# RWKV-7 mixer of a two-layer trunk: chunk loads, PSUM hand-over and the order of paired matmuls

## The chip, the cores and the metric

The kernel runs as one program on one core of a Trainium2 chip. The metric is device microseconds of one execution. Engines are named as in the profile: PE is TensorE, PEld its weight loads, DVE is VectorE, ACT is ScalarE, POOL is GpSimd, SP is SyncE, which here only issues DMAs. A letter q behind an engine (SPq) marks its instruction queue.

## The reference

The network has two layers on 1024 tokens of width 1024: layer 0 mixes with an RG-LRU block, layer 1 with RWKV-7 time mixing; each layer then has cross-attention into 256 memory tokens and a squared-ReLU MLP. The change lies in the RWKV-7 mixer (16 heads of 64):

```python
w_log = -softplus(-(w0 + tanh(xw @ w1) @ w2)) - 0.5      # decay
a = sigmoid(a0 + (xa @ a1) @ a2)
def step(state, inp):                                     # one token, one head
    sa = einsum('bhij,bhj->bhi', state, a_t)
    state = state * w_t + sa * b_t + v_t * k_t
    y_t = einsum('bhij,bhj->bhi', state, r_t)
...
bonus = sum(rh * kh * r_k, axis=-1) * vh
out = (group_norm(y) + bonus) * g
return out @ w_o
```

## The kernel before

Activations lie with channels on the partitions, in eight tiles f of 128 channels (two heads of 64 each, one on partitions 0 to 63, one on 64 to 127) by 1024 tokens. Large products go through `mm3` (L314 to L320): each fp32 operand is split by `split` (L228) into a rounded part and a rest, both fp32r, ACT making the first (L233) and DVE the second (L234), and three fp32r matmuls make one product. Products with few columns use plain fp32 matmuls. SBUF tiles of 128x1024 come from one pool, `u`, with 45 buffers.

The mixer runs in stages. The k stage makes for each f the decay and the gate a (`decay`, L1297): four `mm3` with 64 rows each, w from partitions 0 to 63 and a from 64 to 127, two halves of 512 tokens each, every product followed by a tanh on ACT (L1306); in the program both halves of w come first, then both of a. An r stage follows, and beside both a triangular solve on POOL and DVE, whose results `merge` (L1439) joins on PE. The v stage then makes v for [0, 1], 2, ..., 7. Its `evac_v` (L1526) copies v out of PSUM (L1529), turns it (L1545), forms the product pr of r, k and r_k (L1536), sums pr over the 64 channels of a head with a block matrix of ones as a plain fp32 matmul of 512 columns (L1562), multiplies by v (L1563), makes the gate g (`mm3`, L1566, L1567) and stores the results from SP (L1552, L1556, L1570). `early` loads pr and k ahead (L1575, L1577).

The scan runs over 16 chunks c of 64 tokens. Chunks are loaded from DRAM in pairs n: `load` (keys and b, L1598, four DMAs; a and r, L1601, two), `load_solved` (the solved triangle, L1612), `load_late` (v, L1625; the gates, L1629). `scan_gram` (L1644) makes the 128x128 Gram matrices of a chunk in two groups g of four q: for each q one plain fp32 matmul (L1652) per head h, on partitions 0 to 63 and 64 to 127, into two PSUM banks; `scan_mask` (L1662 on DVE, L1664 on ACT) masks them, `scan_keys` (L1676, L1677) transposes the scaled keys. In the loop over c the steps are `values` (L1757, L1759), `from_state` (L1769), `solved` (L1775, DVE L1777), `update` (L1782, DVE L1784), `output` (L1789, ACT L1791); `post_var` (L1688) and `post_norm` (DVE L1696) normalise the chunk before, `flip_out` (PE L1703, DVE L1708) transposes the one before that. In chunk c the Gram matrices, keys and masks of chunk c + 1 are made.

Tile's scheduler sets the order on each engine from the program's order, the data, free buffers and its own times. `self.line(name)` adds edges: what is issued in the block comes behind the last instruction of the block of that name before, on the same engine; the steps of the loop over c stand in the line "scan". `self.behind()` puts a block's instructions behind the last one issued so far on their engine.

[...] `psum_layout("mixed")` gives four single banks ("still") and two pairs; "banks" closes the pairs' pool and gives four more single banks. The scan uses "banks", and the output projection `tphase` behind it (`p = self.psum()`, L601) uses pairs, after "mixed".

Of the kernel before, what the change touches and what calls it, by code (L numbers as in the profile page):

```python
# [8 lines left out]
F32R = mybir.dt.float32r  # L9
# [1127 lines left out]
def rwkv_consts(self):  # L1137
    nc = self.nc
    c = self.const
    self.omu = c([128, 48], "omu")  # L1140
    nc.vector.tensor_scalar(self.omu, self.colv("mu", 48), -1.0, 1.0, ALU.mult, ALU.add)
    self.w0h = c([128, 8], "w0h")
    nc.vector.tensor_scalar(self.w0h, self.colv("w0"), 0.5, None, ALU.mult)
    self.a0h = c([128, 8], "a0h")
    nc.vector.tensor_scalar(self.a0h, self.colv("a0"), 0.5, None, ALU.mult)
    self.kah = c([128, 8], "kah")
    nc.vector.tensor_scalar(self.kah, self.colv("k_a"), 0.5, None, ALU.mult)
    self.kam = c([128, 8], "kam")
    nc.vector.tensor_scalar(self.kam, self.colv("k_a"), -1.0, 1.0, ALU.mult, ALU.add)
    self.nkk = c([128, 8], "nkk")  # L1150
    nc.vector.tensor_scalar(self.nkk, self.colv("k_k"), -1.0, None, ALU.mult)

    self.ind = c([128, 2], "ind")
    nc.gpsimd.memset(self.ind, 0.0)
    nc.gpsimd.memset(self.ind[0:64, 0:1], 1.0)
    nc.gpsimd.memset(self.ind[64:128, 1:2], 1.0)

    self.id64 = c([128, 64], "id64")
    nc.vector.tensor_add(self.id64, self.ident[:, 0:64], self.ident[:, 64:128])

    self.mask = c([128, 128], "mask")
    nc.gpsimd.memset(self.mask, 1.0)
    for h in range(2):
        r = slice(h * 64, h * 64 + 64)

        for i in range(2):
            m = self.mask[r, i * 64:i * 64 + 64]
            nc.gpsimd.affine_select(m, m, pattern=[[1, 64]], base=i - 1,
                                    channel_multiplier=-1, compare_op=ALU.is_ge, fill=0.0)
    self.db = c([128, 256], "db")  # L1170
    self.pc = c([128, 128], "pc")

    self.ones = c([128, 128], "ones")
    nc.gpsimd.memset(self.ones, 0.0)
    for h in range(2):
        nc.gpsimd.memset(self.ones[h * 64:h * 64 + 64, h * 64:h * 64 + 64], 1.0)

    self.center = c([128, 128], "center")
    nc.vector.scalar_tensor_tensor(self.center, self.ones, -1.0 / 64, self.ident, ALU.mult, ALU.add)

# [60 lines left out]
def rwkv(self, X, xt, lw_wa, lw_g, post, mid):  # L1241
    nc, I = self.nc, self.I
    mm = nc.tensor.matmul
# [17 lines left out]
    wa2 = self.split(raw)  # L1261
    xk, xr, xv = ([[], []] for _ in range(3))
    for hf in range(2):
# [13 lines left out]
        if hf:  # L1277
            h = maps[0][2]
# [18 lines left out]
    def decay(f):  # L1297
        cs = slice(f * 128, f * 128 + 128)
        c1 = lambda t: t[:, f:f + 1]
        lw, a = self.unit(), self.unit()  # L1300
        for t, r, b in ((lw, slice(0, 64), self.w0h), (a, slice(64, 128), self.a0h)):
            for hf in range(2):
                s = slice(hf * 512, hf * 512 + 512)
                p = self.bank()
                self.mm3(p, (wa2[0][r, cs], wa2[1][r, cs]), (hwa[0][r, s], hwa[1][r, s]), True, True)
                nc.scalar.activation(t[:, s], p, AF.Tanh, bias=c1(b), scale=0.5)  # L1306
        nc.vector.tensor_scalar(lw, lw, -LC, -LC, ALU.mult, ALU.add)
        if f > 1:
            nc.scalar.activation(a, a, AF.Copy, scale=0.5, bias=0.5)
        else:  # L1310
            nc.vector.tensor_scalar(a, a, 0.5, 0.5, ALU.mult, ALU.add)
        IP = self.unit()
        nc.vector.tensor_tensor_scan(IP, d01, lw, 0.0, ALU.mult, ALU.add)
        P = lw
        nc.scalar.activation(P, IP, AF.Exp)
        nc.scalar.activation(IP, IP, AF.Exp, scale=-1.0)
        nc.sync.dma_start(Pd[cs, :], P)
        nc.scalar.copy(self.pc.rearrange("p (c q) -> p c q", q=8)[:, :, f], P[:, 63::64])
        dk[f] = a, P, IP
# [206 lines left out]
    def evac_v(f, p):  # L1526
        cs = slice(f * 128, f * 128 + 128)
        vt = self.unit()
        nc.scalar.copy(vt, p)  # L1529
        if f == 1:  # L1530

            self.depth, self.ahead = DA
            with self.behind():
                self.advance(self.taken - 1)
        pr, kp = ld.pop(f)
        nc.vector.scalar_tensor_tensor(pr, pr, self.col("r_k", f), kp, ALU.mult, ALU.mult)  # L1536


        if f % 2 == 0:
            vk[:] = [self.unit() for _ in range(2)]  # L1540
        for e in range(2):
            pt = self.bank()
            for i in range(4):
                tt = e * 4 + i
                mm(pt[:, i * 128:i * 128 + 128], vt[:, tt * 128:tt * 128 + 128], self.center, start=True, stop=True)  # L1545
            nc.scalar.copy(vk[e].rearrange("p (t h g i) -> p t h g i", h=2, g=2, i=64)[:, :, :, f % 2, :],
                           pt.rearrange("p (t h i) -> p t h i", h=2, i=64))
            if f % 2 and e == 0:

                for d in range(2):  # L1550
                    for h in range(2):
                        nc.sync.dma_start(sv0[d][hr[1 - h], h * 512 + (f - 1) * 64:h * 512 + (f + 1) * 64],  # L1552
                                          vk[0].rearrange("p (t h i) -> p t h i", h=2, i=128)[hr[d], 0, h, :])
            if f % 2:
                for h in range(2):
                    nc.sync.dma_start(Vd[e * 512:e * 512 + 512, h, (f - 1) * 64:(f + 1) * 64].rearrange("(t p) i -> p t i", p=128),  # L1556
                                      vk[e].rearrange("p (t h i) -> p t h i", h=2, i=128)[:, :, h, :])
        g1 = self.unit()
        for e in range(2):
            s = slice(e * 512, e * 512 + 512)  # L1560
            bp = self.bank()
            mm(bp, self.ones, pr[:, s], start=True, stop=True)  # L1562
            nc.vector.tensor_mul(vt[:, s], vt[:, s], bp)  # L1563
            gp = self.bank()
            self.mm3(gp, (g2[0][:, cs], g2[1][:, cs]), (hg[0][:, s], hg[1][:, s]), True, True)
            nc.scalar.activation(g1[:, s], gp, AF.Copy, scale=self.col("gn_g", f))  # L1566
            nc.vector.scalar_tensor_tensor(vt[:, s], vt[:, s], self.col("gn_b", f), gp, ALU.add, ALU.mult)  # L1567
        for src, dst in ((g1, G1d), (vt, G2d)):
            for h in range(2):
                nc.sync.dma_start(dst[(f % 2) * 64:(f % 2) * 64 + 64, (f // 2) * 2 + h, :], src[h * 64:h * 64 + 64, :])  # L1570
# [73 lines left out]
    def scan_gram(c, g):  # L1644

        if c >= 16:
            return
        s = cst[c]
        s["pv", g] = [self.bank(h).rearrange("p (q w) -> p q w", q=4) for h in range(2)]
        for q in range(4):  # L1650
            for h in range(2):
                mm(s["pv", g][h][:, q, :], s["st"][g][hr[h], q].rearrange("p w t -> p (w t)"), s["mv"][hr[h], 4 * g + q],  # L1652
                   start=True, stop=True)

    def scan_mask(c, g):
        if c >= 16:
# [58 lines left out]
    for i, fs in enumerate(turns):  # L1715
        for f in turns[i + 1] if i < 6 else []:
            early(f)
        if fs[-1] >= 5:
            self.depth, self.ahead = min(2, 7 - fs[-1]), 0
        self.fphase(I["b_w_rkv"][0, 2], fs, xv, evac_v, spread=i == 0)  # L1720
        aside(len(TURNS) + 6 + i)
        if fs[-1] == LD:
            with self.behind():
                load(0)
        if fs[-1] == 6:
            load_solved(0)
    for c in range(2):
        scan_scale(c)
        for g in range(2):
            scan_gram(c, g)  # L1730
            scan_mask(c, g)
            scan_keys(c, g)
    load_late(0)
    self.psum_layout("banks")
    for h in range(2):
        nc.gpsimd.memset(cst[0]["sv"][hr[h], :, h, :], 0.0)
    for c in range(16):
        if c % 2 == 0:
            with (ExitStack() if c else self.behind()):
                load(c // 2 + 1)  # L1740
                load_solved(c // 2 + 1)
                load_late(c // 2 + 1)
        s = cst[c]
        sv, mv, pcc, xtc, pcs = s["sv"], s["mv"], s["pcc"], s["xt"], s["pcs"]
# [50 lines left out]
        todo = [(decayed, 0), (decayed, 1)] if c < 15 else []  # L1795
        if c:
            todo += [(scan_scale, c + 1)]
        todo += [(values, 0), (from_state, 0)]
        if c > 1:
            todo += [(flip_out, c - 2)]  # L1800
        todo += [(values, 1), (from_state, 1)]
        if c:
            todo += [(post_var, c - 1)]
        todo += [(solved, 0), (solved, 1)]
        if c:
            todo += [(scan_gram, c + 1, 0)]
        if c < 15:
# [14 lines left out]
    post_var(15)  # L1822
    post_norm(15)
    self.depth, self.ahead = 2, 3
    self.psum_layout("mixed")

    self.later += [lambda: flip_out(14), lambda: flip_out(15)]
    w = I["b_w_o"][0]
# [54 lines left out]
```

## Time and profile before

| | us |
|---|---|
| median of 3 runs | 2896.13 |
| lowest and highest run | 2890.81, 2898.02 |
| profiled execution | 2897.32 |
| its span from first to last instruction | 2895.6 |
| mean granted PE clock | 0.987 |
| PE busy in the span | 2804.9 (97%) |

The profiled execution is 1.7 us longer than its span, which is what lies around the first and the last instruction, and 1.2 us above the median. Shares of busy time are averages over many stages; the rows below take the stages of the mixer one by one.

### The profile page before, as it was taken

To read this page: it belongs to the slowest core of one execution; us is meant where nothing else is said; L and a number is where in the kernel's file an instruction comes from. 1 tells how busy PE (TensorE), PEld (TensorE's weight loads), DVE (VectorE), ACT (ScalarE), POOL (GpSimd) and SP (SyncE) were. 2 spreads that over 40 slices of the span, in tenths; PEclk is the share of its full clock that TensorE was granted. 3 is DMA by queue.
4 is the path that set the end of the run, shared out by engine and by line. 5 is a ranking of instruction groups with operands and counts; after the bars stand their busy time and mean duration, and the time that the engine had idled before them with its cause. 6 is when DMAs were issued, how large, how long until landed. Compare 5 with 4: busy or idle time off the path is not lost.

```text
span 2895.6 us, 42717 instructions
## 1 busy us (share of the span) xinstructions
PE 2804.9 (97%) x16955; PEld 2341.9 (81%) x16955; DVE 1834.2 (63%) x1995; ACT 1421.7 (49%) x2195; POOL 907.3 (31%) x962
## 2 busy tenths in 40 slices
PE   7999999999999999999999999999999999999998
PEld 6888788887888888887877777888788788888886
DVE  5577566657455577886675724775665645567778
ACT  5455354546454543347561634564463645454333
POOL 2000114023666500012288113753202276650001
PEclk9999999999999999999999999999999999999999
DMA  8212342323444654442657898952232354464443
GB/s 260 73 50 74 109 161 74 111 80 96 154 148 156 224 183 155 151 136 83 172 142 210 224 231 237 231 146 88 88 95 73 109 163 154 138 243 162 151 175 116
DMA packets 383592, 421.92 MB, mean 146 GB/s; under 512 B 91184, under 2 KB 294176, under 8 KB 383392
## 3 DMA queue, kind: packets, MB, share of 16 engines
q1 hardware_dynamic: 371360, 379.19, 43.5%
q0 software_dynamic: 11568, 39.41, 3.8%
q8 instruction: 133, 2.18, 0.3%
q14 instruction: 67, 0.55, 0.1%
q10 hardware_dynamic: 464, 0.59, 0.1%
HBM read 283.79 MB, written 134.74 MB: 145 GB/s over the span
## 4 chain that ended last, share of the span: by engine, by line
PE 86%; DVE 5%; ACT 3%; DMA 2%; issue 2%; SPq 1%; POOL 0%; DVEq 0%; POOLq 0%; ACTq 0%
PE q L318 17%; PE q L320 17%; PE q L319 17%; PE p L318 9%; PE p L320 9%; PE p L319 9%; DVE u L234 1%; PE q L1652 1%; ACT u L233 1%; PE q L386 1%; DMA u<-in_b_w_rkv 1%; DVE u L1199 1%; PE q L1545 1%; PE q L1769 1%; ACT u L930 1%
## 5 line engine op out<-in xcount | busy, mean ns | idle before, releaser
L234 DVE TENSOR_TENSOR u<-u,u 128x1024 fp32r<-128x1024 f32 (+1 forms) x594 | 799.3, 1378 | 353.9 <-ACT u L233 331.8
L233 ACT CAST u<-u 128x1024 fp32r<-128x1024 f32 (+1 forms) x594 | 582.2, 1019 | 416.3 <-DVE u L1042 224.7
L318 PE MATMUL q<-u,u 128*128 128x512 f32 (+2 forms) x1984 | 760.3, 386 | 15.4 <-ACT u L391 10.0
L319 PE MATMUL q<-u,u 128*128 128x512 f32 (+2 forms) x1984 | 759.6, 384 | 0.5 <-POOL u L366 0.5
L320 PE MATMUL q<-u,u 128*128 128x512 f32 (+2 forms) x1984 | 753.9, 384 | 0.8 <-DVE u L234 0.8
L318 PE MATMUL p<-u,u 128*128 128x512 f32 (+1 forms) x1472 | 557.0, 381 | 12.2 <-ACT u L233 5.4
L319 PE MATMUL p<-u,u 128*128 128x512 f32 (+1 forms) x1472 | 553.1, 376 | 3.7 <-DVE u L234 3.6
L320 PE MATMUL p<-u,u 128*128 128x512 f32 (+1 forms) x1472 | 552.6, 376 | 3.6 <-DVE u L234 3.6
L318 PEld LDWEIGHTS q<-u,u 128*128 128x128 f32 (+1 forms) x1984 | 373.6, 189 | 92.8 <-ACT u L391 10.9
L320 PEld LDWEIGHTS q<-u,u 128*128 128x128 f32 (+1 forms) x1984 | 373.9, 189 | 74.3 <-DVE u L234 1.0
L329 POOL TENSOR_SCALAR s<-s 128x1 f32<-128x1 f32 x98 | 39.0, 398 | 1258.3 <-ACT u L327 1256.7
L319 PEld LDWEIGHTS q<-u,u 128*128 128x128 f32 (+1 forms) x1984 | 374.2, 189 | 72.3 <-POOL u L366 1.0
L318 PEld LDWEIGHTS p<-u,u 128*128 128x128 f32 x1472 | 281.2, 191 | 66.4 <-ACT u L233 7.5
L319 PEld LDWEIGHTS p<-u,u 128*128 128x128 f32 x1472 | 281.3, 191 | 55.0 <-DVE u L234 6.7
L320 PEld LDWEIGHTS p<-u,u 128*128 128x128 f32 x1472 | 281.3, 191 | 54.7 <-DVE u L234 5.2
L440 POOL TENSOR_TENSOR u<-u,u 128x512 f32<-128x512 f32 x120 | 189.1, 1579 | 9.0 <-PE q L319 5.1
L1100 DVE TENSOR_TENSOR z<-z,q 128x512 f32<-128x512 f32 x192 | 130.5, 683 | 81.0 <-PE q L320 81.0
L318 PE MATMUL q<-z,u 128*128 128x512 f32 x320 | 124.7, 391 | 1.6 <-ACT u L233 1.6
L320 PE MATMUL q<-z,u 128*128 128x512 f32 x320 | 124.5, 390 | 1.1 <-DVE u L234 1.1
L319 PE MATMUL q<-z,u 128*128 128x512 f32 x320 | 124.6, 389 | 0.0
L441 POOL TENSOR_TENSOR u<-u 128x512 f32<-128x512 f32 x40 | 70.0, 1749 | 166.1 <-DVE u L234 63.7
L997 POOL TENSOR_TENSOR u<-u,u 128x512 f32<-128x512 f32 x32 | 44.2, 1381 | 177.0 <-ACT u L986 159.8
(247 smaller groups left out, 3334.6 us busy)
## 6 DMA issues: line engine op xcount, KB each, us to landing
u<-d SPq DMA_DIRECT2D x194, 512.0 KB, 4.7
d<-u SPq DMA_DIRECT2D x109, 512.0 KB, 3.5
d<-u POOLq DMA_DIRECT2D x68, 512.0 KB, 3.3
d<-u SPq DMA_DIRECT2D x132, 256.0 KB, 3.6
u<-in_m_w_up SPq DMA_DIRECT2D x64, 512.0 KB, 5.5
u<-in_m_w_down SPq DMA_DIRECT2D x64, 512.0 KB, 8.1
u<-in_c_w_kv SPq DMA_DIRECT2D x32, 512.0 KB, 6.5
u<-in_b_w_rkv SPq DMA_DIRECT2D x24, 512.0 KB, 6.2
```

The costliest lines, as they stand in the source:

```text
L233: self.nc.scalar.copy(hv, src)
L234: (eng or self.nc.vector).tensor_tensor(lv, src, hv, ALU.subtract)
L318: mm(o, ah, bh, start=first, stop=False, **kw)
L319: mm(o, ah, bl, start=False, stop=False, **kw)
L320: mm(o, al, bh, start=False, stop=last, **kw)
L329: nc.gpsimd.tensor_scalar(v, ss, 1.0 / n, eps, ALU.mult, ALU.add)
L386: nc.tensor.transpose(p[:, i * 128:i * 128 + 128], x[:, k * 128:k * 128 + 128], self.ident)
L440: sub = lambda o, x, y: nc.gpsimd.tensor_tensor(o, x, y, ALU.subtract)
L441: nc.gpsimd.tensor_tensor(s[:, a], f1[:, a], f1[:, b], ALU.add)
L930: nc.scalar.activation(e[:, s], p[:, s], AF.Exp, bias=mx[:, i:i + 1], scale=1.0 / 16.0, accum_out=sm[:, i:i + 1])
L997: tt(s1, r21, r22, ALU.add)
L1100: nc.vector.tensor_add(to_, to_, o)
```

## The change

- `decay` goes over the halves of the tokens first, takes two PSUM banks, and issues the three matmuls of w and of a in turn (w, a, w, a, w, a), each matmul in its own block of a line "decay".
- In `scan_gram` each matmul stands in its own block of a line "gram", so that they keep the program's order, which alternates between the heads.
- `evac_v` splits pr into two fp32r tiles and sums each with an fp32r copy of the ones (`ones_r`), accumulating in PSUM.
- `load(1)` moves from chunk 0 of the scan to the v stage, behind v tile 6; `load_solved(1)` stands behind the v stage; both were issued in chunk 0.
- In the loop over c `flip_out` moves from between the two groups of `values` to behind `solved`.
- `psum_layout("mixed")` moves from behind the scan to the start of chunk 15.

```diff
+    self.ones_r = self.cpool.tile([128, 128], F32R, name="ones_r", tag="ones_r")
+    nc.vector.tensor_copy(self.ones_r, self.ones)
...
-        for t, r, b in ((lw, slice(0, 64), self.w0h), (a, slice(64, 128), self.a0h)):
-            for hf in range(2):
-                s = slice(hf * 512, hf * 512 + 512)
-                p = self.bank()
-                self.mm3(p, (wa2[0][r, cs], wa2[1][r, cs]), (hwa[0][r, s], hwa[1][r, s]), True, True)
+        for hf in range(2):
+            s = slice(hf * 512, hf * 512 + 512)
+            ps = [self.bank() for _ in range(2)]
+            for n, (i, j) in enumerate(((0, 0), (0, 1), (1, 0))):
+                for p, r in zip(ps, hr):
+                    with self.line("decay"):
+                        mm(p, wa2[i][r, cs], hwa[j][r, s], start=n == 0, stop=n == 2)
+            for t, p, b in zip((lw, a), ps, (self.w0h, self.a0h)):
                 nc.scalar.activation(t[:, s], p, AF.Tanh, bias=c1(b), scale=0.5)
...
+        prs = self.split(pr)
...
-            mm(bp, self.ones, pr[:, s], start=True, stop=True)
+            for i in range(2):
+                mm(bp, self.ones_r, prs[i][:, s], start=i == 0, stop=i == 1)
...
-                mm(s["pv", g][h][:, q, :], s["st"][g][hr[h], q].rearrange("p w t -> p (w t)"), s["mv"][hr[h], 4 * g + q],
-                   start=True, stop=True)
+                with self.line("gram"):
+                    mm(s["pv", g][h][:, q, :], s["st"][g][hr[h], q].rearrange("p w t -> p (w t)"), s["mv"][hr[h], 4 * g + q],
+                       start=True, stop=True)
...
             load_solved(0)
+            load(1)
+    with self.behind():
+        load_solved(1)
...
     for c in range(16):
+        if c == 15:
+            self.psum_layout("mixed")
         if c % 2 == 0:
             with (ExitStack() if c else self.behind()):
-                load(c // 2 + 1)
-                load_solved(c // 2 + 1)
+                if c:
+                    load(c // 2 + 1)
+                    load_solved(c // 2 + 1)
                 load_late(c // 2 + 1)
...
-        todo += [(values, 0), (from_state, 0)]
-        if c > 1:
-            todo += [(flip_out, c - 2)]
-        todo += [(values, 1), (from_state, 1)]
+        todo += [(values, 0), (from_state, 0), (values, 1), (from_state, 1)]
         if c:
             todo += [(post_var, c - 1)]
         todo += [(solved, 0), (solved, 1)]
+        if c > 1:
+            todo += [(flip_out, c - 2)]
...
     self.depth, self.ahead = 2, 3
-    self.psum_layout("mixed")
```

## Rows read from the trace of the kernel before

**Rows 1.** The page: shares of the chain that ended last, by engine
```profile
PE 86%; DVE 5%; ACT 3%; DMA 2%; issue 2%; SPq 1%; POOL 0%; DVEq 0%; POOLq 0%; ACTq 0%
```
**Rows 2.** Windows: stretch, length, busy us (instructions) per engine, granted clock, DMA share, GB/s
```profile
1356.00:1464.00 108.00, 108.00 (x718) 86.32 (x716) 71.87 (x71) 69.16 (x94) 33.71 (x41) 0.98 0.57 155
...
1600.00:1764.00 164.00, 156.56 (x1398) 122.44 (x1397) 71.84 (x103) 74.17 (x106) 33.36 (x50) 0.98 0.83 221
1764.00:1924.00 160.00, 153.45 (x3088) 138.08 (x3086) 112.05 (x212) 86.93 (x360) 107.44 (x123) 0.98 0.98 226
1924.00:1949.00 25.00, 21.05 (x191) 16.93 (x188) 19.47 (x23) 17.93 (x52) 4.95 (x5) 0.86 0.37 106
1786.50:1793.40 6.90, 6.22 (x58) 5.58 (x59) 2.92 (x6) 0.89 (x2) 4.88 (x6) 0.51 0.98 228
1933.30:1940.10 6.80, 6.12 (x27) 4.77 (x24) 5.45 (x6) 6.00 (x21) 1.83 (x2) 0.50 0.29 93
...
1745.00:1760.00 15.00, 13.90 (x125) 10.97 (x126) 2.87 (x5) 4.71 (x7) 7.00 (x9) 1.00 0.47 142
```
**Rows 3.** Timeline of PE, decay matmuls: start, us, operation, count
```profile
1371.61 0.49 PE L318 MATMUL q<-u,u 64*128 64x512 f32 x1
...
1372.19 0.62 PE L318 MATMUL q<-u,u 64*128 64x512 f32 x2
...
1373.77 0.50 PE L318 MATMUL p<-u,u 128*128 128x512 f32 x1
...
1399.86 0.50 PE L318 MATMUL q<-u,u 64*128 64x512 f32 x1
...
1400.66 0.39 PE L318 MATMUL q<-u,u 64*128 64x512 f32 x1
1400.89 0.39 PE L319 MATMUL q<-u,u 64*128 64x512 f32 x1
...
1401.44 0.50 PE L319 MATMUL p<-u,u 128*128 128x512 f32 x1
```
**Rows 4.** Timeline of PE, Gram matmuls of the scan
```profile
1764.71 1.71 PE L1652 MATMUL q<-z,u 64*128 64x128 f32 x16
...
1809.48 1.16 PE L1652 MATMUL q<-z,u 64*128 64x128 f32 x16
...
1812.70 1.71 PE L1652 MATMUL q<-z,u 64*128 64x128 f32 x16
```
**Rows 5.** The chain in order of time, and ACT's timeline, both of the v stage
```profile
1669.68 0.86 PE q L1562 x2
...
1722.68 1.04 ACT L233 CAST u<-u 128x1024 fp32r<-128x1024 f32 x1 [10.76 <-DMA u<-in_b_w_rkv]
```
**Rows 6.** Timelines of PE and of SP's queue around chunks 1 and 2
```profile
1787.18 2.08 PE L1652 MATMUL q<-z,u 64*128 64x128 f32 x16 [3.73 <-issue]
...
1795.78 0.64 PE L1757 MATMUL q<-u,u 128*64 128x64 f32 x16
...
1780.49 6.25 SPq L1598 DMA_DIRECT2D u<-d  x4
...
1797.01 6.91 SPq L1598 DMA_DIRECT2D u<-d  x4
```
**Rows 7.** Timelines of PE, DVE and ACT in the loop over chunks
```profile
1807.32 0.69 PE L1757 MATMUL q<-u,u 128*64 128x64 f32 x16
...
1816.79 0.63 PE L1703 MATMUL q<-ident,u 128*128 128x128 f32 x4 [0.22 <-DVE u L1696]
...
1924.48 0.33 PE L1757 MATMUL q<-u,u 128*64 128x64 f32 x2 [0.41 <-ACT u L1664]
...
1805.13 0.77 DVE L1696 TENSOR_TENSOR u<-u,g 128x512 f32<-128x512 f32 x1
...
1811.30 1.77 DVE L1784 TENSOR_TENSOR u<-u,q 64x256 f32<-64x256 f32 x4 [0.29 <-PE q L1782]
...
1815.62 0.40 ACT L1664 COPY u<-z 64x256 f32<-64x256 f32 x1 [0.19 <-DVE u L1662]
```

## The prediction

> **What bounds the kernel now.** I read the page's chain first, then windows of the mixer's stages, then the timelines of the places that the change touches. PE is 86% of the chain that ended last [rows 1], so a microsecond taken from PE's queue counts wherever PE has no wait behind which it vanishes. The windows say where that is so. While the decays run, PE is busy 108.00 of 108.00 us; in the v stage 156.56 of 164, in the scan 153.45 of 160, and at the change to the output projection 21.05 of 25 [rows 2]. [...] The scan has a second candidate: its DMA share is 0.98 [rows 2].
>
> **Decays.** A decay is twelve matmuls of 64 rows by 512 columns. In the row's order two of one half of the partitions follow each other at 0.23 us (1400.66 to 1400.89), and six of them take 1.58 us to the next matmul, that is 6 x 0.23 = 1.38 and 0.2 for going in and out of the 64-row shape [rows 3]. Where w's second product meets a's first, a row of two appears, and twelve take only 2.16 us (1371.61 to 1373.77) instead of 2.96: a pair from the two halves of the partitions runs in the time of one [rows 3]. The trace has eight groups of six, three of twelve, one of nine (1.59) like the former and one of three (0.9): 12.6 + 6.5 + 1.6 + 0.9 = 21.6 us for eight decays. In turns, every matmul has its partner: 3 x 0.23 + 0.2 = 0.9 us for each half of the tokens, 16 x 0.9 = 14.4 us, or 8 x (6 x 0.23 + 0.2) = 12.6 if the halves stay together. The gain is 7.2 to 9.0 us; I take 7.2, since most groups stand alone now. If pairs are torn apart it falls to 5. Nothing is added on ACT. The work hidden beside is none: PE is full here, and the DMAs of this stage (share 0.57 [rows 2]) hold nothing up.
>
> [...]
>
> **Bonus sums.** Each of the 16 plain fp32 matmuls of 512 columns takes 0.86 us on the chain [rows 5]; two fp32r matmuls of the same size take 2 x 0.23 = 0.46 [rows 3]. That is 16 x 0.40 = 6.4 us off PE. The price is per v tile one cast on ACT (1.04 [rows 5]) and one subtraction on DVE, and two more `u` buffers. ACT is busy 74.17 of these 164 us and DVE 71.84 [rows 2], so they fit. But ACT works in order, and once it sits 10.76 us before a cast that waits for a weight's DMA [rows 5], with v tiles' evacuations behind it; one more cast in that queue is 1.0 us of PE's wait, and the first tile, where pr comes just ahead of its matmul, waits for cast and subtraction once. I take 4.5 us; the ends are 1 and 6.4.
>
> **Gram matrices.** Eight fp32 matmuls, 16 records, take 1.71 us in some groups and 1.16 in others [rows 4]. In the shorter ones both heads start together, in the longer ones one head's four come first. The difference is 0.55 us. Of 32 groups 17 have the longer order: the four of chunks 0 and 1 ahead of the loop (from 1764.71 [rows 4]), and the second group of each of the chunks 2 to 14, that of chunk 2 at the lower clock. The first four give 4 x 0.55 = 2.2 us.
>
> In the loop the gain meets the next bound. From values(0) of chunk 2 at 1795.78 to that of chunk 15 at 1924.48 there are 13 periods of 9.90 us [rows 6, 7]; in 12 of them 0.55 would come off PE, and 0.22 more where `flip_out` waits for `post_norm` [rows 7], which its new place ends. The loop through DVE and ACT is: update's additions start at 1811.30, the last mask's copy on ACT ends at 1816.02, so values(1) can start 4.8 us later; from values(1) at 1807.32 to those additions are 3.98 us, now without `flip_out`, which is 0.63 long and is put into just this stretch [rows 7]. 4.8 + 3.98 + 0.63 = 9.4 us. So this loop, not PE, sets the period, and the gain is 13 x (9.90 - 9.40) = 6.5 us. If `post_norm` (0.77 at 1805.13, then one more mask [rows 7]) comes ahead of the last mask, 0.68 is added and the gain is nothing; by PE's work alone it would be 12 x 0.55 and some of the 0.22, 8 us.
>
> **The second pair of chunks.** PE stands 3.73 us before chunk 2's first Gram matrices [rows 6], and of the 6.22 busy us in the window behind it, at clock 0.51, up to half, 3.1 us, is the price of the lower clock [rows 2]. What it waits for is in SP's queue: the four DMAs of `load(1)` are issued from 1780.49 on, behind the last v tile's stores [rows 6], and PE goes on 6.7 us after the first. In its new place `load(1)` is behind v tile 6, where from 1745 to 1760 the DMA share is 0.47 [rows 2], so it lands 20 us ahead of its use. The stall goes, 3.73 + 3.1 = 6.8 us. What is late next is pair 2: its first DMA goes out at 1797.01 and lands by the same 6.7 us at 1803.7, for matmuls at 1809.48 [rows 4, 6], 5.8 us early; these come 10 us sooner now, but the queue ahead of it is shorter by 6.25 us and `load_solved`, so some 3 us are left. Moved past on SP are the last tile's own loads and stores; the copies into the first chunk's state may slip by the 6.25 us of the four issues. I take 6.0; ends 0 and 6.8.
>
> **PSUM one chunk sooner.** From 1924 to 1949 PE is idle 25 - 21.05 = 3.95 us, and the half clock of 1933.30 to 1940.10 costs about half of its 6.12 busy us, 3 [rows 2]. With a pair of banks free during chunk 15 the projection's first matmuls can fill these gaps. But they need split weights, DVE is busy 19.47 of the 25 us and ACT 17.93 with them [rows 2], and chunk 15 has four banks in place of eight. I take 3.0; ends 0 and 6.9.
>
> **Sum.** 7.2 + 4.5 + 2.2 + 6.5 + 6.0 + 3.0 = 29.4 us off the profiled 2897.3, gives 2867.9. That execution lies 1.2 us above the median of the runs shown, so I forecast 2867. With the low ends (5, 1, 2.2, 0, 0, 0: 8.2 us) 2888, with the high ones (9.0, 6.4, 2.2, 8, 6.8, 6.9: 39.3 us) 2857.
>
> **Rivals.** (1) The scan is bound by its transfers. For: DMA share 0.98 and 226 GB/s over the stage, at best 5.8 us between landing and use [rows 2, 4, 6]. Then a shorter period only moves the wait: the stall reappears before the Gram matrices of chunk 4, and the loop's 6.5 and the stall's 6.0 are gone: 29.4 - 12.5 = 16.9, 2879. Against: from pair to pair the queue now gains on PE, with waits in it for buffers that PE frees.
>
> (2) The turns do not overlap, because the second bank is late or the scheduler puts other matmuls between: 7.2, 2.2 and 6.5 fall away, 13.5 are left, 2883. For: four banks. Against: both kinds of pairs are in the trace already [rows 3, 4].
>
> (3) `post_norm` stays ahead of the last mask: without the loop's 6.5, 2873.
>
> (4) Slower. The `u` pool runs short in the v stage: two buffers for pr per tile and four for `load(1)` and `load_solved(1)` stand while weights are still to be fetched, so a tile's weights come one tile late. Its price is the 10.76 us which ACT sits before such a cast [rows 5], of which PE sees the part that its own queue doesn't cover, 3.7 us as at chunk 2, and 3 us for the lower clock behind it. One such stall costs 6.7 us; five more use up the 29.4, and with all six of the single v tiles it is 40 against 29.4: 2907. It decides from the fifth stall on. Against: by v tile 6, where `load(1)` stands, no weights beyond tile 7 are to come, and the trace has one such stall in the stage.
>
> **Chances.** Forecast 0.58; (1) 0.15; (3) 0.12; (2) 0.10; (4) 0.05. The range from 2855 to 2888 takes in the first four with their own spread. A difference under 0.3%, 8.7 us, can't be told from no change: below 2887.4 is faster, to which the forecast gives nearly all of its chance, (1) and (3) nine tenths and (2) six tenths: 0.86. Slower 0.05, the rest, 0.09, is the same.
>
> **What would show it.** Decays: twelve matmuls or six in rows of two, 0.9 us per half. Bonus: 32 fp32r matmuls on the line of L1562, 0.46 us per pair. Gram: 1.16 us in all 32 groups. Loop: a period of 9.4 us, with DVE and ACT without a gap from update's additions to the last mask; 9.9 would be rival (3) or (1), and for (1) PE's waits would name a DMA. Stall: no idle time over 1 us and clock 1.00 through chunks 1 and 2. Hand-over: projection matmuls between chunk 15's. For (4): ACT's casts waiting for `in_b_w_rkv` in several tiles. The prediction is wrong if the gain is under 9 us, or if it is large but from a place that isn't in the sum, such as another order of the scheduler in a stage that the change doesn't touch.

## The result

The changed kernel takes 2889.96 us (median of 13 runs) against 2896.13 us before, a ratio of 0.9977 with a 95% interval of 0.9966 to 0.9987. So it is faster, but by 6.2 us where 29.4 were forecast. That is less than the 8.7 us that I took for the least that can be told from no change, and the time lies 2 us above the top of my range. Between the two profiled spans (2895.6 and 2886.8 us) the gain is 8.8 us. The views after that answer to those of before are these: the chain's shares on the page, then the windows by stage (stretch, length, busy us and instructions of each engine, granted clock, DMA share, GB/s).

```profile
PE 83%; DVE 5%; DMA 3%; ACT 3%; POOL 2%; SPq 2%; issue 2%; DVEq 0%; POOLq 0%; ACTq 0%
```
```profile
1352.00:1460.00 108.00, 107.40 (x733) 82.85 (x732) 72.58 (x74) 72.27 (x100) 31.54 (x40) 1.00 0.53 147
1492.00:1549.00 57.00, 42.80 (x226) 34.31 (x227) 50.30 (x45) 32.05 (x44) 52.09 (x57) 0.85 0.49 142
1608.00:1764.00 156.00, 144.99 (x1366) 117.31 (x1365) 79.33 (x109) 79.74 (x111) 33.39 (x50) 0.98 0.88 235
1764.00:1918.00 154.00, 146.91 (x3040) 130.36 (x3040) 109.51 (x208) 89.70 (x364) 104.36 (x122) 1.00 0.99 233
1918.00:1943.00 25.00, 23.08 (x270) 18.81 (x266) 22.37 (x29) 19.00 (x54) 8.73 (x8) 1.00 0.37 107
```

PE's share of the chain fell by 3 points to the benefit of POOL, DMA and SP's queue [rows 1]. The clock of 0.86 at the hand-over is 1.00 now [rows 2]. But the second row is a stretch that my rows do not hold, the change from the k to the r stage. The same stretch before:

```profile
1492.00:1549.00 57.00, 53.86 (x348) 43.91 (x347) 45.44 (x42) 28.17 (x38) 50.79 (x61) 0.97 0.61 174
```

PE is busy 11 us less there, does 226 matmuls instead of 348, and the clock is 0.85. Setting the same instruction of both traces side by side, place by place, gives this account (us, minus is a gain; the expectations quoted below still count 0.8 us of the last v tile among the Gram groups, hence their 4.3 and 2.0, and give the stall 4.8):

| place | forecast | measured in the trace |
|---|---|---|
| k stage with the decays | -7.2 | -4.1 |
| change from k to r, 1492 to 1549 | 0 | **+14.2** |
| rest of the r stage | 0 | -2.2 |
| v stage with the bonus sums | -4.5 | -5.1 |
| first four Gram groups | -2.2 | -1.2 |
| stall at chunk 2 | -6.0 | -3.9 |
| chunks 2 to 14 | -6.5 | -0.9 |
| last chunk and hand-over | -3.0 | -4.6 |
| behind it | 0 | -1.0 |
| sum | -29.4 | -8.8 |

### The profile page after: what moved, and what is told of

It is laid out like the page before. It is cut to its first block, busy times and chain, and to the rows that moved or that the text cites. A ratio compares the mean times of both kernels' runs of the same rounds, so it can differ in the third digit from the quotient of the medians.

```text
span 2886.8 us, 42719 instructions
## 1 busy us (share of the span) xinstructions
PE 2781.7 (96%) x16955; PEld 2319.8 (80%) x16955; DVE 1840.0 (64%) x2004; ACT 1431.4 (50%) x2203; POOL 912.7 (32%) x962
## 3 DMA queue, kind: packets, MB, share of 16 engines
q8 instruction: 133, 2.18, 0.3%
## 4 chain that ended last, share of the span: by engine, by line
PE 83%; DVE 5%; DMA 3%; ACT 3%; POOL 2%; SPq 2%; issue 2%; DVEq 0%; POOLq 0%; ACTq 0%
PE q L320 16%; PE q L318 16%; PE q L319 16%; PE p L318 9%; PE p L320 9%; PE p L319 9%; DVE u L234 2%; DMA u<-in_b_w_rkv 2%; ACT u L233 1%; PE q L1661 1%; PE q L386 1%; POOL u L1417 1%; POOL w L1415 1%; DMA u<-d 1%; DVE u L417 1%
## 5 line engine op out<-in xcount | busy, mean ns | idle before, releaser
L234 DVE TENSOR_TENSOR u<-u,u 128x1024 fp32r<-128x1024 f32 (+1 forms) x602 | 807.6, 1374 | 353.8 <-ACT u L233 327.1
L233 ACT CAST u<-u 128x1024 fp32r<-128x1024 f32 (+1 forms) x602 | 591.0, 1020 | 434.2 <-DVE u L1042 224.8
L318 PE MATMUL q<-u,u 128*128 128x512 f32 (+1 forms) x1952 | 745.4, 384 | 15.7 <-ACT u L391 10.0
L319 PE MATMUL q<-u,u 128*128 128x512 f32 (+1 forms) x1952 | 747.0, 383 | 1.7 <-DVE u L234 1.2
L320 PE MATMUL q<-u,u 128*128 128x512 f32 (+1 forms) x1952 | 741.2, 383 | 0.8 <-DVE u L234 0.8
L318 PE MATMUL p<-u,u 128*128 128x512 f32 (+1 forms) x1472 | 555.6, 380 | 25.8 <-DVE u L1332 10.2
L318 PEld LDWEIGHTS q<-u,u 128*128 128x128 f32 x1952 | 367.4, 188 | 89.3 <-ACT u L391 10.9
L319 PEld LDWEIGHTS q<-u,u 128*128 128x128 f32 x1952 | 367.5, 188 | 74.2 <-DVE u L234 3.1
L320 PEld LDWEIGHTS q<-u,u 128*128 128x128 f32 x1952 | 367.2, 188 | 72.7 <-DVE u L234 1.0
```

Of the source, the lines that this page charges most:

```text
L233: self.nc.scalar.copy(hv, src)
L234: (eng or self.nc.vector).tensor_tensor(lv, src, hv, ALU.subtract)
L318: mm(o, ah, bh, start=first, stop=False, **kw)
L319: mm(o, ah, bl, start=False, stop=False, **kw)
L320: mm(o, al, bh, start=False, stop=last, **kw)
```

## Where the 14 us went

ACT's timeline in that stretch, first after, then before. L1427 after and L1421 before are the copy in `solve_store(0)`; L233 are casts of the next stage's weights.

```profile
1482.16 2.09 ACT L1427 COPY u<-u 64x1024 f32<-64x1024 f32 x1 [12.61 <-POOL u L1417]
1484.15 1.05 ACT L233 CAST u<-u 128x1024 fp32r<-128x1024 f32 x1
1491.54 1.04 ACT L233 CAST u<-u 128x1024 fp32r<-128x1024 f32 x1 [6.34 <-DMA u<-in_b_w_rkv]
```
```profile
1482.50 2.08 ACT L1421 COPY u<-u 64x1024 f32<-64x1024 f32 x1 [11.47 <-POOL u L1411]
1484.45 2.01 ACT L233 CAST u<-u 128x1024 fp32r<-128x1024 f32 x2
```

In both kernels the copy waits for POOL, whose solve ends at 1482: what PE saves before that does not move POOL. Before, two casts follow at once. After, the second waits 6.34 us more for its weights. SP's queue says why, first after, then before (L1428 and L1422 store the solved chunk, L249 loads weights):

```profile
1477.19 0.58 SPq L1395 DMA_DIRECT2D d<-u  x1
1482.15 0.34 SPq L1428 DMA_DIRECT2D d<-u  x1
1484.27 0.48 SPq L1429 DMA_DIRECT2D d<-u  x1
1484.84 2.12 SPq L249 DMA_DIRECT2D u<-in_b_w_rkv  x2
```
```profile
1475.68 1.23 SPq L249 DMA_DIRECT2D u<-in_b_w_rkv  x1
...
1483.11 0.56 SPq L1422 DMA_DIRECT2D d<-u  x1
1484.60 0.48 SPq L1423 DMA_DIRECT2D d<-u  x1
1485.17 0.54 SPq L249 DMA_DIRECT2D u<-in_b_w_rkv  x1
```

Before, one of the two weight loads went out at 1475.68, ahead of the stores. After, the scheduler put the stores first; SP stands idle from 1477.8 until POOL is done, with both loads behind it. The late cast makes PE wait in its turn (1502.00, then four more waits of 0.7 to 1.6 us), with spells of 10.2 us, most of it idle, and 6.8 us at half clock (the granted clock is 0.50 from 1494.95 to 1505.19 and from 1532.50 to 1539.33):

```profile
1502.00 0.77 PE L318 MATMUL p<-u,u 128*128 128x512 f32 x1 [10.24 <-DVE u L1332]
```

My theory T1 was that the decays' shorter matmuls flip this order. Five runs stand for it or against it. All ratios below are to the kernel before; its own median moved between 2893.9 and 2897.3 us from series to series, so the ratios compare better than the times.

**e1_old_decay** undoes the decays.

```diff
-        for hf in range(2):
-            ps = [self.bank() for _ in range(2)]
-            ...
+        for t, r, b in ((lw, slice(0, 64), self.w0h), (a, slice(64, 128), self.a0h)):
+            for hf in range(2):
+                self.mm3(p, (wa2[0][r, cs], wa2[1][r, cs]), (hwa[0][r, s], hwa[1][r, s]), True, True)
```


> The changed kernel with the decays' matmuls put back as they were (three matmuls of one map, then three of the other); everything else of the change stays. Theory T1: the decays' shorter k stage let the order of SP's instructions flip, so that two weight loads of the r stage stand behind the stores of the first solved chunk, which wait for POOL; that loses 14.2 us between 1492 and 1547 us of the changed kernel's trace. With the old decays the second of these loads goes ahead of the stores again: k stage 4.1 us longer, the 14.2 us stall gone (0 lost there against the kernel before), the later gains (v stage 4.3, first Gram groups 2.0, chunk 2's stall 4.8, hand-over 4.6) stay: 2896.1 - 16.7, some 2880 (2876 to 2884). Rival R1 (the loss belongs to another edit, such as the buffers that the bonus sums' split parts or the constant of ones take): the loss stays and only the decays' gain goes, some 2894 (2891 to 2897).

2883.2 us, 0.9953 (0.9941 to 0.9966): taking a gain away made the kernel 6.7 us faster. In its trace one weight load goes ahead of the stores again (L1425 is the first store):

```profile
1477.46 0.74 SPq L249 DMA_DIRECT2D u<-in_b_w_rkv  x1
...
1484.53 0.56 SPq L1425 DMA_DIRECT2D d<-u  x1
```

**e2_only_decay** is the kernel before with the decays alone (the diff above, reversed).


> The kernel before with the decays' edit alone. T1: 4.1 us gained in the k stage, then 12 to 14 us lost in the change to the r stage: 2896.1 + 8 to + 10, some 2904 (2901 to 2907), slower than before by 0.3%, with weight casts of ACT waiting for a transfer near 1490 us of the trace. R1: the loss belongs to another edit and is not here, so that the decays' gain remains, some 2892 (2889 to 2894).

2900.7 us, 1.0021 (1.0011 to 1.0030): slower, by 6 us (forecast 8 to 10). ACT shows the same wait as after, and PE stands 9.98 us at 1502.46:

```profile
1482.84 2.08 ACT L1424 COPY u<-u 64x1024 f32<-64x1024 f32 x1 [12.59 <-POOL u L1414]
1484.82 1.06 ACT L233 CAST u<-u 128x1024 fp32r<-128x1024 f32 x1
1492.21 1.04 ACT L233 CAST u<-u 128x1024 fp32r<-128x1024 f32 x1 [6.34 <-DMA u<-in_b_w_rkv]
```

From 1488 to 1564 us its trace loses 11.2 us on the kernel before, where the changed kernel loses 14.2. So it is the decays' edit and no other; R1 falls. What in this edit turns the scheduler's order, the shorter time, the edges of the line "decay" or the second bank, was not tried.

**e3_store_later** gives out the stores one turn later.

```diff
-SL, SO, ST = (2, 5, 8, 9), (2, 5, 8, 9), (5, 8, 12, 13)
+SL, SO, ST = (2, 5, 8, 9), (2, 5, 8, 9), (6, 8, 12, 13)
```


> The changed kernel with the first solved chunk's copy and stores given out one turn later (the first number of ST 6 in place of 5), all of the change in place. T1: both weight loads of that turn go ahead of the stores and ACT's casts are not held up, the 14.2 us between 1492 and 1547 us go, and the 4.1 us of the decays stay: 2890.0 - 10 to - 14, some 2877 (2873 to 2882). R1: the loss has nothing to do with where the stores stand: 2890 (2886 to 2894).

2876.9 us, 0.9936 (0.9924 to 0.9948), as T1 has it.

**e4_before_later** is its control: the same line in the kernel before.


> The kernel before with the first solved chunk's copy and stores one turn later: the control for the run above. T1: the kernel before had one weight load behind the stores and its two casts ran late by no more than some 2 us of PE's idle time (gaps of 1.73 and 1.29 us at 1509 and 1526 us): 2893 to 2896, no change that can be told or a little faster. R1': if turning the stores later is worth 10 us by itself, whatever the decays do, this kernel is faster by as much: some 2885.

2898.3 us, 1.0006 (0.9995 to 1.0016): no difference. The edit is worth 12 (by the ratios) to 13 us only where the decays have turned the queue.

**e13_pool_queue** moves nothing but the queue of the two stores; ACT's order stays.

```diff
+        dma = (nc.sync if q else nc.gpsimd).dma_start
-        nc.sync.dma_start(Xd[q]...)
+        dma(Xd[q]...)
```


> The changed kernel (2890.0 us), the first solved chunk's stores issued by POOL, which solves it, in place of SP; its copy stays where it is, in front of ACT's two weight casts. Theory T1 (the head of SP's queue): the weight loads no longer stand behind a store that waits for POOL, the second cast runs right behind the copy, and the loss between 1492 and 1547 us goes although ACT waits 12 us for POOL's solve as before: 2877 (2873 to 2882), as with the stores one turn later. Rival R8 (the head of ACT's queue: the casts are late because the copy waits there): nothing moves, 2890 (2887 to 2893), and the run store later gained because it moved the copy too.

2882.1 us, 0.9957 (0.9943 to 0.9971), at the upper end of T1's span. The second cast follows at once although the copy still waits 11.9 us, PE's wait falls from 10.24 to 1.95 us, and at the end of that change the kernel is 11.0 us ahead of the changed one. Then it gives 5.3 us back, 3.9 of them where the first merge waits for the same store, which now stands behind the next solve in POOL's queue (issued at 1543.18):

```profile
1477.09 1.20 SPq L249 DMA_DIRECT2D u<-in_b_w_rkv  x2
```
```profile
1480.63 2.08 ACT L1427 COPY u<-u 64x1024 f32<-64x1024 f32 x1 [11.88 <-POOL u L1417]
1482.61 2.00 ACT L233 CAST u<-u 128x1024 fp32r<-128x1024 f32 x2
```
```profile
1492.91 0.47 PE L318 MATMUL p<-u,u 128*128 128x512 f32 x1 [1.95 <-DVE u L1332]
...
1571.49 0.28 PE L1455 MATMUL q<-u 32*32 32x32 f32 x2 [3.90 <-DMA u<-d]
```

So SP's queue carries 11 of the 14 us. This kernel trails e3 there by the other 3; they are probably the copy's, at the head of ACT's queue, but no run moves the copy alone.

## The loop over chunks

The time from one chunk's `update` to the next, for chunks 2 to 14 (us; worked out from the traces):

| kernel | undisturbed turns, even and odd | chunks 2 to 14 |
|---|---|---|
| before | 9.77, 10.03 | 119.9 |
| changed | 9.37, 9.70 | 119.0 |
| store later | 9.37, 9.70 | 115.6 |
| store later, one pool | 9.37, 9.37 | 114.1 |
| store later, Gram order free | 9.98, 9.74 | 121.5 |
| store later, flip at its old place | 10.10, 10.16 (two even turns 9.51) | 121.7 |

The 9.4 us that I worked out as the loop's limit is there in every second turn. In the others the second Gram group waits in its middle. Timelines of the run with the stores later (PE, PE's weight loads, DVE):

```profile
1798.77 1.77 DVE L1799 TENSOR_TENSOR u<-u,q 64x256 f32<-64x256 f32 x4 [0.16 <-PE q L1797]
...
1800.14 0.29 PEld L1661 LDWEIGHTS q<-z,u 64*128 64x128 f32 x2 [0.17 <-DVE u L1799]
1800.14 1.66 PE L1661 MATMUL q<-z,u 64*128 64x128 f32 x16
...
1809.84 1.16 PE L1661 MATMUL q<-z,u 64*128 64x128 f32 x16
```

Its first head starts; its second does not until DVE's last addition, which ends at 1800.54, has freed the bank. The group takes 1.59 us to the next line instead of 1.09.

**e5_one_pool** (this run and e6 to e11 stand on e3_store_later):

```diff
-        yp = self.bank(c)
+        yp = self.bank(0)
-        p = self.bank(c + 1)
+        p = self.bank(1)
```


> The changed kernel with the stores one turn later (as in the run store later, 2876.9 us, ratio 0.9936) and one edit more: a chunk's output sum always takes its bank from the first PSUM pool and the turned chunk's from the second, where now they swap with the chunk's parity. Theory T2: in every second turn of the scan the second Gram group takes 1.60 us in place of 1.09, since its second head's bank is the one that the state's update held until DVE's last add; with this edit each pool serves five tiles a turn in the same order and the bank comes from an earlier user: all second groups 1.09 us, seven turns by 0.5 us, some 3.5 us less, 2873.4 (2872 to 2875). Rival R2: DVE and ACT set the turn's length, so a faster group only moves PE's wait to the next place: 2877 (2876 to 2878).

2878.3 us, 0.9942 (0.9925 to 0.9960): no better than 0.9936 as a whole. In the trace the mechanism is as T2 says: each second group is 1.16 us long, nine of the twelve turns take 9.37, and from chunk 0's update to chunk 14's it gains 3.0 us on e3. But its profiled execution comes to the scan 4.6 us late, from spells of half clock in stages whose program is the same (mean granted clock of the execution 0.990, in e3's 0.993). So the gain is shown in the turns, and not in the time.

```profile
1800.12 1.16 PE L1661 MATMUL q<-z,u 64*128 64x128 f32 x16
1803.32 1.16 PE L1661 MATMUL q<-z,u 64*128 64x128 f32 x16
```

**e6_gram_free** undoes the Gram order.

```diff
-                with self.line("gram"):
-                    mm(s["pv", g][h][:, q, :], ...)
+                mm(s["pv", g][h][:, q, :], ...)
```


> As store later (2876.9 us), with the Gram matmuls' order left to the scheduler as in the kernel before. T2: the first four groups go from 1.29 (mean) back to 1.64 us (+1.2 us, a little more with the half clock), and the second group of each turn from 1.09 or 1.60 to 1.64 us (seven turns by 0.55, some +3.9): 2882 (2880 to 2883). Rival R2 (the loop is set by DVE and ACT): only the first four groups come back, 2878 (2877 to 2879).

2878.7 us, 0.9946 (0.9930 to 0.9962); the interval holds both values. In the trace the groups of 1.71 are back, and chunk 14's update comes 2.9 us later than in e3: chunks 2 to 14 take 5.9 us more, but this run comes to chunk 2 with 3.0 us less of the wait that e3 has there.

**e10_old_flip** puts `flip_out` back between the halves of the values.

```diff
+        if c > 1:
+            todo += [(flip_out, c - 2)]
         todo += [(values, 1), (from_state, 1)]
...
-        if c > 1:
-            todo += [(flip_out, c - 2)]
```


> As store later (2876.9 us), with the turning of chunk c - 2 back at its old place between the two halves of the values. T6: the flip's four matmuls are the same work anywhere in the turn, and the turns' gain belongs to the Gram matmuls' order: 2877 (2875.5 to 2878.5). Rival R6: at its old place DVE's product of the turned chunk stands ahead of the solved state's products in DVE's queue and holds the update back by some 0.4 us a turn, so that the new place carries most of the loop's gain: 14 turns by 0.4, some 2882 (2880 to 2884).

2880.6 us, 0.9956 (0.9942 to 0.9969): R6's time, but by another wait than it names. In nine turns PE waits 0.35 to 0.66 us before the flip for `post_norm` (L1705), which DVE takes behind the last mask, and from chunk 0's update to chunk 14's it takes 6.5 us longer than e3:

```profile
1834.24 0.66 PE L1712 MATMUL q<-ident,u 128*128 128x128 f32 x4 [0.66 <-DVE u L1705]
```

So the undisturbed turns are 9.90 us on average before, 9.86 with the flip's place alone, 10.13 with the Gram order alone (chunks 5 to 13), and 9.53 with both: the gain needs both edits, and the Gram order alone loses.

The changed kernel has one thing more: PE stops in the middle of a line, with no semaphore to wait for.

```profile
1892.40 0.75 PE L1790 MATMUL q<-u,u 64*64 64x64 f32 x20
1895.06 0.56 PE L1790 MATMUL q<-u,u 64*64 64x64 f32 x12 [1.91 <-issue]
...
1906.60 0.80 PE L1797 MATMUL q<-u,u 128*64 128x64 f32 x18
1908.56 0.68 PE L1797 MATMUL q<-u,u 128*64 128x64 f32 x14 [1.16 <-issue]
```

From chunk 2 on there are three such stops, 3.8 us; the kernel before has one of 0.67, e3 none. The DMA records suggest a cause. Packets of 16 KB of the queue that the page calls "instruction" (q8: 133 packets, 2.18 MB in the whole execution) come in the scan every 6 us on average. The 12 packets from 1818.1 to 1882.4 us of the changed kernel stand 5.84 us apart, and at 947 matmuls and 946 weight loads in 45 us (the window below) PE runs 246 instructions in that time. The packets at these two stops came 9.7 and 8.9 us after the one before, and PE went on 1.7 and 1.3 us after they ended. In the scans of all fifteen kernels there are 25 stops of over 0.45 us of this kind, and at every one PE goes on 1.3 to 1.7 us after the end of such a packet.

**e12_less_traffic** tests this on the changed kernel.

```diff
-        for w in range(2):
+        for w in range(2 if n < 4 else 0):
             nc.sync.dma_start(mv[:, :, w, :], MVd[:, :, w, ts])
```


> The changed kernel with the loads of the matrices of keys and receptances left out for the pairs of chunks 4 to 7 (1 MB of some 4 MB for each pair); these chunks compute with the matrices of four pairs before. Nothing else is left out. Theory T8: PE's stops of 0.7 to 1.9 us in the middle of one line, with no semaphore to wait for, come when its next 16 KB of instructions arrive late behind the scan's transfers: the stops at 1895 and 1908 us of the changed kernel (3.1 us together) have no like here, no turn from the eighth on is longer than 10.0 us, and the scan from chunk 2's update to chunk 14's takes 115 us where it took 119.0: 2886 (2883 to 2889). Rival R9 (the stops belong to the place in the program or to PE itself): stops of over 0.5 us remain from the eighth turn on, and the time is 2890 (2888 to 2892).

2888.0 us, 0.9970 (0.9960 to 0.9980), where the two spans touch; the time decides nothing. Windows of this run, then of the changed kernel:

```profile
1860.00:1905.00 45.00, 44.89 (x965) 40.10 (x961) 33.86 (x67) 27.77 (x122) 36.98 (x42) 1.00 0.64 154
```
```profile
1860.00:1905.00 45.00, 42.98 (x947) 38.63 (x946) 31.83 (x62) 27.51 (x116) 35.83 (x41) 1.00 1.05 232
```

With DMA share 0.64 there is no stop and no turn above 9.94 us from the eighth on; one of 0.84 us is left where the share is still 1.05. That speaks for T8, but e3 had no stop at full traffic in these turns either, and one profile of each is no proof. That PE's stops end shortly behind an instruction packet is shown; that the loads make the packet late is only likely.

## The stall, the hand-over and the bonus sums

**e7_old_load** undoes the second pair's move.

```diff
-            load(1)
-    with self.behind():
-        load_solved(1)
...
-                if c:
-                    load(c // 2 + 1)
-                    load_solved(c // 2 + 1)
+                load(c // 2 + 1)
+                load_solved(c // 2 + 1)
```


> As store later (2876.9 us), with the second pair's loads back behind the last v tile's stores. T3: the stall ahead of chunk 2's first Gram group comes back, by the changed kernel's trace 4.8 us (on record as 6.0): 2882 (2881 to 2884), with PE waiting some 3 us or more for a transfer there. Rival R3 (the stretch is bound by the transfers as a whole, the wait only moves): 2877 to 2878.

2882.3 us, 0.9958 (0.9944 to 0.9972): T3. The profiled execution is 13.5 us above the median, so only the wait itself is read from it, and the slow group behind it: 16 records in 2.08 us, as in [rows 6], where the clock is 0.51 [rows 2]:

```profile
1793.41 2.08 PE L1661 MATMUL q<-z,u 64*128 64x128 f32 x16 [5.38 <-DMA u<-d]
```

**e11_values_ahead** (on e5) asks what is late next at this place.

```diff
     with self.behind():
         load_solved(1)
+        load_v(1)    # the loads of sv, taken out of load_late(1)
```


> The run one pool (output sums in one PSUM pool, stores one turn later) with one edit more: the values of the second pair of chunks are loaded right behind the second pair's solved blocks, ahead of the third pair's matrices and of the first two pairs' factors, some 2 MB of transfers that stand ahead of them now. T7: chunk 2's values then wait for no transfer (1.5 and 0.4 us of PE's idle time and 3.4 us at half clock go there), 2.5 to 3.5 us less than the run one pool: 2870 if that one comes out at 2873. Rival R7: the transfers are at their limit from 1760 to 1800 us, so the wait moves to another load (the grams' or the turned chunk's factors): as the run one pool.

2872.2 us, 0.9924 (0.9905 to 0.9943), the fastest here, though its interval overlaps that of e3. In the changed kernel PE waited 1.33 and 0.30 us for chunk 2's values, in e3 1.49 and 0.41. Here that wait is gone, and from chunk 1's update to chunk 2's it takes 9.37 us, where e5 takes 12.20 and e3 13.55. Of the 7.5 us between its profiled span and e5's, though, 5.9 lie ahead of the scan, where both run the same instructions on PE; so the wait is shown gone, and not that the edit is worth 6 us. So the stall of [rows 6] had two causes in SP's queue, and the change removed the first.

**e8_old_handover** gives PSUM back after the last chunk.

```diff
-        if c == 15:
-            self.psum_layout("mixed")
...
+    self.psum_layout("mixed")
     self.later += [lambda: flip_out(14), lambda: flip_out(15)]
```


> As store later (2876.9 us), with PSUM handed over after the last chunk, as before. T4: the idle time behind the last chunk comes back with its spell of half clock: by the changed kernel's trace 4.6 us at the last turned chunk's matmul (on record as 3.0): 2881.5 (2880 to 2883). Rival R4 (the projection's first matmuls wait for weights or the norm anyway): 2877 to 2878.

2881.6 us, 0.9948 (0.9932 to 0.9964), which looks like T4; but from chunk 14's update to the last flip its trace loses 0.2 us on e3, and to the end of the kernel 1.7. The projection's matmuls wait 0.92 us in this run and 0.51 us in e3:

```profile
1921.20 0.50 PE L318 MATMUL p<-u,u 128*128 128x512 f32 x1 [0.92 <-ACT u L1804]
```
```profile
1916.52 0.50 PE L320 MATMUL p<-u,u 128*128 128x512 f32 x1 [0.51 <-DVE u L234]
```

The kernel before had 1.65 and 0.68 us and the half clock (0.50 from 1933.30 to 1940.10 [rows 2]):

```profile
1931.73 2.33 PE L1789 MATMUL q<-u,u 128*64 128x64 f32 x32 [1.65 <-DVE u L1777]
...
1934.74 0.79 PE L318 MATMUL p<-u,u 128*128 128x512 f32 x1 [0.68 <-ACT u L1791]
```

The wait of 1.65 us for DVE's solved products (L1777) is gone in e8 and in e3: in its new place `flip_out` fills it (first row). But it is gone in e10 too, which has the flip at its old place and PSUM handed over early. There the projection's matmuls stand between chunk 15's, as I had forecast:

```profile
1917.54 0.66 PE L1712 MATMUL q<-ident,u 128*128 128x128 f32 x4
```
```profile
1915.99 0.63 PE L1790 MATMUL q<-u,u 64*64 64x64 f32 x16
1916.94 0.50 PE L318 MATMUL p<-u,u 128*128 128x512 f32 x1 [0.33 <-ACT u L233]
```

From chunk 14's update to the end the kernel before takes 974.9 us, e8 970.9, e10 969.6 and e3 969.3. So either edit alone gives most of the gain, and the 4.6 us can't be put down to one of them.

**e9_old_bonus** undoes the bonus sums.

```diff
-        prs = self.split(pr)
-                mm(bp, self.ones_r, prs[i][:, s], start=i == 0, stop=i == 1)
+            mm(bp, self.ones, pr[:, s], start=True, stop=True)
```


> The changed kernel with the stores one turn later (2876.9 us, ratio 0.9936), and the bonus sums back as one fp32 matmul of 0.86 us each. T5: the v stage loses what the trace of the changed kernel shows it gained, 4.3 us (on record as 4.5; 16 sums by 0.40 us are 6.4): 2881.2 (2880 to 2883). Rival R5 (the split's copies on ACT and the extra buffers cost as much as the sums gave, and the v stage gained by something else): 2877 or less (2874 to 2878).

2882.5 us, 0.9961 (0.9943 to 0.9979): 7 us by ratio, 9.0 in the v tiles of the trace, 10 us at half clock among them (the granted clock is 0.96 from 1633 to 1759 us, in e3 1.00 from 1633 to 1752). T5 in its sign; the size is open, since spells of half clock come and go in this stage, whose clock is 0.98 before [rows 2] and after.

## Why the prediction was wrong

- **The step that failed** is in the decays: "the DMAs of this stage (share 0.57 [rows 2]) hold nothing up". I asked for work hidden beside the matmuls and for the stage's DMA share, not what stands next in SP's and ACT's queues. There it was POOL's solve, which ends at 1482 with or without the decays. In the sum 7.2 us were gained, and the change to the r stage stood at nothing; it lost 14.2 us. By e2 the edit costs 6 us, and without its loss (e3) the kernel is at 2877, inside the range, though 10 us short of the forecast by the terms below.
- **Decays, their size:** 4.1, not 7.2 and even below my low end of 5. Of 16 halves six are torn: the first matmul stands alone (0.43 us to the next instruction), projection matmuls follow, then the other five come in 0.89:

```profile
1393.11 0.96 PE L1310 MATMUL q<-u,u 64*128 64x512 f32 x6
1399.26 0.50 PE L1310 MATMUL q<-u,u 64*128 64x512 f32 x1
1400.34 0.96 PE L1310 MATMUL q<-u,u 64*128 64x512 f32 x5
...
1452.17 1.65 PE L1310 MATMUL q<-u,u 64*128 64x512 f32 x11 [0.60 <-DVE u L1388]
```

  In the last row PE waits 0.60 us in the middle of twelve until DVE (L1388) has freed the second bank; these twelve take 2.68 us, and six at 1444.97, where DVE (L1372) holds the second bank, 1.23. It is rival 2, in the decays and in the second Gram group of every other turn. In the Gram groups and at these two places the second bank is late; what tore the other pairs was not tried.
- **Loop:** 0.9 instead of 6.5. The period of 9.4 was right for half of the turns (0.33 more in the others, 2 us), and the stops took 3.8.
- **Stall:** 3.9 instead of 6.0; the next load was late at once, not after three chunks. That is rival 1 at one place, at chunk 2 only: no wait for a transfer comes back at chunk 4, and most turns of e5 take 9.37 us, so the scan as a whole is not bound by transfers.
- **Bonus sums:** 5.1 for 4.5. **First Gram groups:** 1.2 instead of 2.2. They take 1.62, 1.33, 1.15 and 1.29 us to the next line where they took 1.64; in the first the second head's bank is late here too, held by DVE's L1571.
- **Hand-over:** 4.6 for 3.0. My reason works (e10), but so does the flip's new place (e8), which I had not counted here; in the changed kernel the flip fills the wait. That the size is near is luck.
- **Rival 3** did not happen: `post_norm` runs behind the last mask. **Rival 4** had the right mechanism, ACT's casts waiting for `in_b_w_rkv`, but in the r stage and from the order of a queue, not for want of buffers. I gave it 0.05; a chance for "an edit in one stage turns the order of an in-order queue" should have stood beside it.

## What to carry over

Where a scheduler orders in-order queues, an edit in one stage has to be followed to the next instruction in each queue that waits for an engine that the edit does not touch; here SP stood idle from 1477.8 until POOL's solve ended at 1482. A store that waits for a slow solver belongs behind the loads that others wait for, or in another queue. The pairs of matmuls gained in full only where both banks were free together: a second Gram group takes 1.09 us so, and 1.59 where its second bank is late. Two edits at one loop can each be worth nothing alone and something together (the turns), or each the same as both (the hand-over), so they are tested both ways.

## What the hardware showed beside this

I had not expected PE to stop with no semaphore to wait for and to go on only 1.3 to 1.7 us behind the end of an instruction packet. It did so in the scans of thirteen of the fifteen kernels, the one before among them, for 0.5 to 1.9 us at a time, in a stage whose DMA share is 0.98 before [rows 2] and 0.99 after. Nor had I expected how much a single execution differs: e5 and e8 come to the scan 4.6 and 3.7 us later than e3 with the same instructions on PE until there, with spells of half clock that e3 does not have (mean granted clock of the execution 0.990 and 0.991, in e3 0.993). A term of 3 us is read from the turns of a loop, then, not from the times.
